# Scores and probability transposes of two pairs of heads at a time, both as 64-row products in double PSUM banks

## The chip, the cores and the metric

The kernel runs on one core of one Trainium2 chip. The metric is the device time of one execution in microseconds, as a median of several runs. The engines are TensorE (PE, with its weight loads as PEld), VectorE (DVE), ScalarE (ACT), GpSimd (POOL) and SyncE (SP), which issues nearly all DMAs.

## What is computed

Two layers of a decoder, 256 tokens, width 1024, float32. Each layer normalises its input, projects it with one 1024 x 9808 matrix, runs three causal attention mixers of eight heads of 64 (a: plain causal, b: only the 64 keys that an indexer selects per query, c: with a forgetting bias), gates and projects each, merges them by gates, projects once more and adds to the residual; a last RMSNorm ends it.

```python
h = rms_norm(x, gain)
proj = jnp.einsum('bsd,de->bse', h, w_in)
...
rel = jax.nn.relu(jnp.einsum('bqhd,bsd->bqhs', qi, k_idx))
isc = jnp.einsum('bqh,bqhs->bqs', wi, rel).astype(jnp.float32)
ival, idx = lax.top_k(isc, top)
...
s = jnp.einsum('bqhd,bkhd->bhqk', qc, kh).astype(jnp.float32) * scale
p = jax.nn.softmax(s, axis=-1).astype(v.dtype)
return jnp.einsum('bhqk,bhkd->bqhd', p, vh)
...
merged = jnp.sum(gates * y, axis=2)
return x + jnp.einsum('bsd,de->bse', merged, w_out)
```

## The kernel before

Every float32 matmul with weights is done as three products of split operands: high part by high part, high by low and low by high. ACT makes the high part of a weight block (`wh`, L371), DVE the low part (`wl`, L375), both into rings of six. A unit of projection is 24 matmuls of 128 x 256 into one PSUM bank of a ring of three (`proj`, L419). Units of gates and output projections (`unit_m`, `unit_y`) are strewn among those of the mixers by `between`, so that PE has other work while a softmax runs.

The work is not issued in the order in which it is written. Each `pe`, `act`, `dve`, `gps` and `dma` call adds an operation to a `Plan`, with its dependences, a key and a cost in ns. `Plan.run` walks through them, always takes the engine that can start earliest and there the ready operation with the lowest key, and emits it: so the costs (`QK` and numbers in the calls), a margin of 200 ns on some PE operations, and the numbers of buffers set each engine's order, which is then fixed. Buffers of one name are handed out in the order in which they were made.

Heads go in pairs, since two heads of 64 fill 128 partitions. For a pair, `scores` (L579 to L591) makes twelve products: for the first 128 queries against 128 keys, then for the next 128 against 256 keys, three split products each, for both heads in turn; one head uses rows 0 to 63 of PE, the other rows 64 to 127, and each its own PSUM bank (`s`, two banks). Then DVE adds the bias and takes a maximum (L650), ACT makes the exponentials (L654), DVE a reciprocal (L657), DVE or ACT the normalisation (L664, L661). The probabilities of a head, 128 x 384, are turned by three 128 x 128 transposes on PE (L676) into a bank of `t` (two banks). ACT copies them out as the high part (`pth`, L679), DVE makes the low part (`ptl`, L681); of both there is one buffer for a pair. Four matmuls a head (L693 to L696) then weigh the values into `o`, one bank. The indexer's four pairs of heads use `scores` too, followed by a ReLU on ACT (L805) and sums on DVE (L816).

A mixer's units of a half (two pairs) come as q, q, g, g, k, k: after a key unit its pair's attention is queued (`attend`). At the end, `forms` (L1070) issues sixteen transposes of 64 rows, two at a time for the two halves of PE, whose results nobody reads.

## Time and profile before

| | us |
|---|---|
| median of 3 runs | 608.72 (608.58 to 608.77) |
| profiled execution, its own time | 609.18 |
| its span, first to last instruction | 607.4 |
| PE busy | 600.0 |
| DVE busy | 525.5 |
| ACT busy | 401.0 |
| granted TensorE clock | 0.998 |

Busy times are unions of an engine's instruction times. Matmuls overlap, so what one costs is read from start to start. The chain of waits follows the work that ended last back to its beginning; idle time of an engine outside it costs nothing.

### The profile page before, as it was taken

Reading aid. Unit: us, or ns where it says so; the run is one execution under the profiler, and the core shown is the slowest. Engines: PE = TensorE matmul, PEld = TensorE weight load, DVE = VectorE, ACT = ScalarE, POOL = GpSimd, SP = SyncE. Lnnn points to the kernel's source line nnn. Section 1 sums busy time; section 2 is a strip of 40 time slices with the busy share of each in tenths; the row PEclk is TensorE's granted clock in tenths of the full one; section 3 lists DMA queues with packets and bytes.
Section 4 is the critical chain, followed back from the end, with each engine's and each line's share of the span. In section 5 each row is a group of like instructions: output and inputs, shape, how many; then the busy total and the mean of one; then the engine's idle time right before and its main releaser. Section 6 shows DMA issues by size and latency. Waiting matters only on the chain.

```text
span 607.4 us, 12894 instructions
## 1 busy us (share of the span) xinstructions
PE 600.0 (99%) x5036; PEld 576.3 (95%) x5036; DVE 525.5 (87%) x1227; ACT 401.0 (66%) x813; POOL 85.1 (14%) x98
## 2 busy tenths in 40 slices
PE   9999999999999999999999999999999999999996
PEld 8999999989998999999889999999999999999995
DVE  6799999787889989979588899987869898999783
ACT  6785568495777667775587563957768674858641
POOL 1232022200000223200003312202000013330001
PEclk9999999999999999999999999999999999999999
DMA  9767464736472654455555828283564556453811
GB/s 306 254 209 250 139 217 160 244 105 202 146 241 73 208 175 144 153 198 201 161 175 172 278 74 253 92 281 102 184 198 147 166 175 208 140 174 105 278 36 69
DMA packets 94461, 107.68 MB, mean 177 GB/s; under 512 B 4400, under 2 KB 82496, under 8 KB 94400
## 3 DMA queue, kind: packets, MB, share of 16 engines
q1 hardware_dynamic: 94112, 106.47, 54.8%
q8 instruction: 39, 0.64, 0.4%
q10 hardware_dynamic: 288, 0.39, 0.2%
q14 instruction: 22, 0.18, 0.1%
HBM read 105.79 MB, written 1.06 MB: 176 GB/s over the span
## 4 chain that ended last, share of the span: by engine, by line
PE 89%; DVE 7%; issue 1%; ACT 1%; DMA 1%; POOL 0%; POOLq 0%; ACTq 0%; SPq 0%
PE proj L419 75%; PE s L588 4%; PE t L676 3%; DVE wl L375 2%; PE proj L973 2%; DVE isc L837 1%; DMA raw<-in_w_in_dram 1%; PE t L898 1%; DVE t L836 1%; PE o L696 1%; PE o L693 1%; ACT wh L371 1%; PE o L694 0%; PE o L695 0%; DVE isc L816 0%
## 5 line engine op out<-in xcount | busy, mean ns | idle before, releaser
L375 DVE TENSOR_TENSOR wl<-raw,wh 128x1024 fp32r<-128x1024 f32 (+1 forms) x190 | 236.3, 1252 | 37.3 <-ACT wh L371 34.4
L371 ACT ACTIVATE wh<-raw 128x1024 fp32r<-128x1024 f32 (+1 forms) x190 | 199.8, 1057 | 85.0 <-PE proj L419 53.0
L419 PE MATMUL proj<-hTh,wh 128*128 128x256 f32 (+1 forms) x1040 | 247.5, 277 | 0.0
L419 PE MATMUL proj<-hTl,wh 128*128 128x256 f32 (+1 forms) x1040 | 245.6, 275 | 0.0
L419 PEld LDWEIGHTS proj<-hTh,wh 128*128 128x128 f32 (+1 forms) x1040 | 198.9, 191 | 1.2 <-DVE g L620 0.3
L419 PEld LDWEIGHTS proj<-hTl,wh 128*128 128x128 f32 (+1 forms) x1040 | 199.0, 191 | 0.1
L419 PE MATMUL proj<-hTh,wl 128*128 128x256 f32 (+1 forms) x1040 | 161.6, 278 | 0.0
L419 PEld LDWEIGHTS proj<-hTh,wl 128*128 128x128 f32 (+1 forms) x1040 | 136.7, 191 | 2.3
L475 POOL TENSOR_TENSOR rsh<-rsh,cst 128x256 f32<-128x256 f32 (+1 forms) x42 | 33.6, 800 | 370.3 <-DVE rsh L474 361.2
L654 ACT ACTIVATE e<-e,st 128x128 f32<-128x128 f32 x96 | 42.6, 445 | 15.6 <-DVE st L650 15.1
L477 POOL TENSOR_TENSOR rr<-rr,rsh 128x256 f32<-128x256 f32 (+1 forms) x42 | 42.8, 1021 | 7.0 <-DVE rr L476 3.8
L419 PE MATMUL proj<-wh,v 128*128 128x512 f32 (+1 forms) x144 | 33.7, 356 | 0.0
L419 PE MATMUL proj<-og0l,wh 128*128 128x256 f32 x128 | 31.9, 275 | 0.0
L419 PE MATMUL proj<-og0h,wh 128*128 128x256 f32 x128 | 31.9, 275 | 0.0
L419 PE MATMUL proj<-wh,hTh 128*128 128x512 f32 x80 | 31.7, 396 | 0.0
L419 PE MATMUL proj<-wh,hTl 128*128 128x512 f32 x80 | 30.5, 382 | 0.2 <-DVE hTl L535 0.2
L419 PEld LDWEIGHTS proj<-wh,v 128*128 128x128 f32 x144 | 25.2, 190 | 2.9
L681 DVE TENSOR_TENSOR ptl<-t,pth 128x384 fp32r<-128x384 f32 x48 | 25.1, 547 | 0.6 <-ACT pth L679 0.5
L419 PE MATMUL proj<-og0h,wl 128*128 128x256 f32 x128 | 24.7, 275 | 0.0
L419 PEld LDWEIGHTS proj<-og0h,wh 128*128 128x128 f32 x128 | 24.6, 192 | 0.0
L419 PEld LDWEIGHTS proj<-og0l,wh 128*128 128x128 f32 x128 | 24.6, 192 | 0.0
L679 ACT ACTIVATE pth<-t 128x384 fp32r<-128x384 f32 x48 | 22.3, 487 | 2.7 <-PE t L676 2.6
(196 smaller groups left out, 978.1 us busy)
## 6 DMA issues: line engine op xcount, KB each, us to landing
raw<-in_w_in_dram SPq DMA_DIRECT2D x74, 1024.0 KB, 5.2
raw<-in_w_branch_dram SPq DMA_DIRECT2D x24, 512.0 KB, 3.8
raw<-in_w_out_dram SPq DMA_DIRECT2D x8, 1024.0 KB, 5.1
brow<-drow SPq DMA_DIRECT2D x4, 512.0 KB, 6.0
raw<-in_w_in_dram SPq DMA_DIRECT2D x3, 512.0 KB, 7.5
x<-in_x_dram SPq DMA_DIRECT2D x4, 256.0 KB, 3.0
raw<-in_w_in_dram SPq DMA_DIRECT2D x2, 320.0 KB, 8.8
out_dram<-tmp SPq DMA_DIRECT2D x2, 320.0 KB, 2.5
```

The costliest lines, as they stand in the source:

```text
L371: ACT.activation(p[0].v, sel(c.v), AF.Copy)
L375: DVE.tensor_tensor(p[1].v, sel(c.v), p[0].v.bitcast(F32), op=ALU.subtract)
L419: PE.matmul(o(), a(), b(), start=first and i == 0, stop=last and i == n - 1)
L475: gps(lambda: POOL.tensor_tensor(T(sh)[:np_], T(sh)[:np_], s[:np_], op=ALU.mult), S, [k_rope], [sh], key, "rope")
L477: gps(lambda: POOL.tensor_tensor(T(r)[:np_], T(r)[:np_], T(sh)[:np_], op=ALU.add), S, [sh], [r], key, "rope")
L588: PE.matmul(T(s)[:, a:a + n].rearrange("p (b a) -> p b a", a=2), st[r, sl], turns(mv[r, :n]), start=i == 0, stop=i == 2, skip_group_check= ...
L654: act(lambda t=t, a=a, n=n, e=e, st=st: ACT.activation(T(e)[:, a:a + n], T(e)[:, a:a + n], AF.Exp, bias=T(st)[:, t:t + 1], scale=-1.0, acc ...
L676: PE.transpose(T(ps)[:, i * 128:(i + 1) * 128], T(es[h])[:, i * 128:(i + 1) * 128], ident)
L679: act(lambda h=h, src=src: ACT.activation(T(ph)[:, h], src(), AF.Copy), 384, True, [ps], [kp[h][0]], key, "pT", touch=[ph])
L681: dve(lambda h=h, src=src: DVE.tensor_tensor(T(pl)[:, h], src(), T(ph)[:, h].bitcast(F32), op=ALU.subtract), 384, [ps, kp[h][0]], [kp[h][1 ...
L693: PE.matmul(o0(128), v[:, 0, hd], f(T(ph), 0), start=True, stop=False, skip_group_check=True)
L973: PE.matmul(T(ps[t]).rearrange("p (b a) -> p b a", a=2), h(2 * i + x, t), turns(v3(w)[:, x]), start=left[t][0] == 23, stop=left[t][0] == 0)
```

## The change

Two pairs are treated together. `scores` no longer queues its products: it returns them as a job, and `half_rows` queues the jobs of two pairs as one PE operation, which the planner prices at the sum of their costs plus one `SWITCH`. Within a pair, the 256-key part comes ahead of the 128-key part. The probabilities of both pairs are transposed by one such operation too, with products of 64 rows: for each 128 x 128 block, rows 0 to 63 and rows 64 to 127 are transposed in turn by the two halves of PE, 12 products a pair, into the two banks of a double bank. PSUM has two double banks `d` in place of the banks `s` and `t`; all their former users take `d`. One ACT copy and one DVE subtraction of 768 columns per pair replace two of 384. The units of a half come as q, q, k, k, g, g, and the attention of both pairs is queued after the second key unit. The indexer's four pairs go in two groups. `forms` is gone. `Bank` objects only tell the planner which engine used a bank last.

```diff
-QK = 700.0
+PARTS = ((0, 6),)
+QK = 672.0
+PT = 360.0
+SWITCH = 330.0
 FB = ("DVE",)
 FBK = 0
-BANKS = ("proj", "s", "t", "o")
+BANKS = ("proj", "o")
...
-    ptag("s", 2)
-    ptag("t", 2)
+    ptag("d", 2, 1024)
     ptag("o", 1)
...
-    def scores(q, k, ktoks, key):
-        s2 = [Buf("s"), Buf("s")]
+    def half_rows(jobs, key, name):
+
+        def go():
+            for f in fs:
+                f()
+        fs, cost, reads, writes, touch = zip(*jobs)
+        pe(go, sum(cost) + SWITCH, [r for x in reads for r in x], [w for x in writes for w in x], key, name, MARGIN,
+           touch=[t for x in touch for t in x])
+
+    def scores(q, k, toks):
+        d = Buf("d")
 
         def go():
             qh, ql = T(q[0]), T(q[1])
             kh, kl = T(k)
-            for a, n, sl in ((0, 128, slice(0, 128)), (128, 256, slice(128, 256))):
+            for a, n, sl in ((128, 256, slice(128, 256)), (0, 128, slice(0, 128))):
                 for i, (st, mv) in enumerate(((qh, kh), (ql, kh), (qh, kl))):
-                    for r, s in zip(HEAD, s2):
-                        PE.matmul(T(s)[:, a:a + n].rearrange("p (b a) -> p b a", a=2), st[r, sl], turns(mv[r, :n]),
+                    for h, r in enumerate(HEAD):
+                        c = h * 512 + a
+                        PE.matmul(T(d)[:, c:c + n].rearrange("p (b a) -> p b a", a=2), st[r, sl], turns(mv[r, :n]),
                                   start=i == 0, stop=i == 2, skip_group_check=True)
-        pe(go, QK, [q[0], q[1], k] + ktoks, s2, key, "qk", MARGIN)
-        return s2
+        return d, (go, QK, [q[0], q[1], k] + toks, [d], d.banks)
+
+    def transposes(es, ke):
+        d = Buf("d")
+
+        def go():
+            for j in range(6):
+                e = T(es[j // 3])[:, (j % 3) * 128:(j % 3 + 1) * 128]
+                for u, r in enumerate(HEAD):
+                    PE.matmul(T(d)[:, u * 512 + j * 64:u * 512 + j * 64 + 64], e[r], ident[r, r], is_transpose=True,
+                              start=True, stop=True, skip_group_check=True)
+        return d, (go, PT, ke + [k_id], [d], es + d.banks)
 
     class Pair:
...
-            self.attend(key + 1)
+            self.key = key + 1
+            if self.p % 2:
+                attend(self.both)
...
+            self.p_es, self.p_ke = es, [k for kk in ke for k in kk]
+
+        def values(self, ps, key):
             ph, pl = Buf("pth"), Buf("ptl")
-            kp = [[Tok(), Tok()] for _ in range(2)]
-            for h in range(2):
-                ps = Buf("t")
-
-                def tr(h=h, ps=ps):
-                    for i in range(3):
-                        PE.transpose(T(ps)[:, i * 128:(i + 1) * 128], T(es[h])[:, i * 128:(i + 1) * 128], ident)
-                pe(tr, 275.0, ke[h] + [k_id], [ps], key, "pT", MARGIN, touch=[es[h]])
-                src = lambda ps=ps: T(ps)[:, :384]
-                act(lambda h=h, src=src: ACT.activation(T(ph)[:, h], src(), AF.Copy), 384, True, [ps],
-                    [kp[h][0]], key, "pT", touch=[ph])
-                dve(lambda h=h, src=src: DVE.tensor_tensor(T(pl)[:, h], src(), T(ph)[:, h].bitcast(F32), op=ALU.subtract),
-                    384, [ps, kp[h][0]], [kp[h][1]], key, "pT", touch=[ph, pl])
+            kp = []
+            for a, n in PARTS:
+                src = lambda a=a, n=n: T(ps).rearrange("p (u c) -> p u c", u=2)[:, :, a * 64:(a + n) * 64].rearrange("p u (j q) -> p j u q", q=64)
+                dst = lambda x, a=a, n=n: T(x).rearrange("p h c -> p (h c)")[:, a * 128:(a + n) * 128].rearrange("p (j u q) -> p j u q", u=2, q=64)
+                k = [Tok(), Tok()]
+                kp.append(k)
+                act(lambda src=src, dst=dst: ACT.activation(dst(ph), src(), AF.Copy), 128 * n, True, [ps], k[:1], key, "pT", touch=[ph] + ps.banks)
+                dve(lambda src=src, dst=dst: DVE.tensor_tensor(dst(pl), src(), dst(ph).bitcast(F32), op=ALU.subtract), 128 * n,
+                    [ps, k[0]], k[1:], key, "pT", touch=[ph, pl] + ps.banks)
...
+    def attend(prs):
+        key = prs[-1].key
+        sc = [scores(p.q, p.k, p.kt) for p in prs]
+        half_rows([j for _, j in sc], key, "qk")
+        for p, (d, _) in zip(prs, sc):
+            p.softmax(d, p.key)
+        ts = [transposes(p.p_es, p.p_ke) for p in prs]
+        half_rows([j for _, j in ts], key, "pT")
+        for p, (d, _) in zip(prs, ts):
+            p.values(d, p.key)
...
-        s2 = scores(q, kb, ktoks, key + 1)
-        base = (p % 2) * 768
-        rel = [tmp6[:, base + h * 384:base + (h + 1) * 384] for h in range(2)]
-        for h in range(2):
-            for a, n in ((0, 128), (128, 256)):
-                act(lambda h=h, a=a, n=n: ACT.activation(plain(rel[h][:, a:a + n]), tiles(T(s2[h])[:, a:a + n]), AF.Relu), n, True, [s2[h]],
-                    [k_tmp[p % 2]], key + 1, "relu")
-        for h in range(2):
-            hd = 2 * p + h
-            for t, (a, n) in enumerate(((0, 128), (128, 256))):
-                rr = rel[h][:, a:a + n]
-                w = widx[:, t, hd:hd + 1]
-                o = isc[:, a:a + n]
-                if hd == 0:
-                    f = lambda rr=rr, w=w, o=o: DVE.tensor_scalar(o, rr, w, None, op0=ALU.mult)
-                else:
-                    f = lambda rr=rr, w=w, o=o: DVE.scalar_tensor_tensor(o, rr, w, o, op0=ALU.mult, op1=ALU.add)
-                dve(f, n, [k_tmp[p % 2], k_widx], [k_isc[t]], key + 1, "isc", t_dve(n) + 76.0, port=True)
+        held.append((p, *scores(q, kb, ktoks)))
+        if p % 2 == 0:
+            return
+        half_rows([j for _, _, j in held], key + 1, "qk")
+        for p, d, _ in held:
+            base = (p % 2) * 768
+            rel = [tmp6[:, base + h * 384:base + (h + 1) * 384] for h in range(2)]
+            for h in range(2):
+                for a, n in ((0, 128), (128, 256)):
+                    act(lambda d=d, h=h, a=a, n=n, rel=rel: ACT.activation(plain(rel[h][:, a:a + n]), tiles(T(d)[:, 512 * h + a:512 * h + a + n]),
+                                                                           AF.Relu), n, True, [d], [k_tmp[p % 2]], key + 1, "relu", touch=[d.banks[h]])
...
-                for hf in range(2) for kind in "qgk" for p in (2 * hf, 2 * hf + 1)]
+                for hf in range(2) for kind in "qkg" for p in (2 * hf, 2 * hf + 1)]
...
-    def forms():
-
-        b = [Buf("s"), Buf("s")]
-
-        def emit():
-            for i in range(8):
-                for r, s in zip(HEAD, b):
-                    PE.matmul(T(s)[:, (i % 4) * 64:(i % 4) * 64 + 64], tmp6[r, i * 128:(i + 1) * 128], ident[r, r], is_transpose=True,
-                              start=True, stop=True, skip_group_check=True)
-        pe(emit, 900.0, [k_main] + k_tmp, b, 10 ** 6, "forms")
-    forms()
```

The planner orders the engines anew. PE, first layer, the first mixer's second half (`L419` and `L428` are projections, `L588` and `L609` scores, `L676` and `L620` transposes); before, the transposes of one pair's two heads and the beginning of the next pair's scores:

```order
L419 MATMUL proj_165<-hTh,wl_70 128x256 x4
L676 MATMUL t_170<-cst,e_136 128x128 x3
L419 MATMUL proj_166<-wh_64,hTh 128x512
L419 MATMUL proj_166<-wh_64,hTl 128x512
L419 MATMUL proj_166<-wh_64,hTh 128x512
L419 MATMUL proj_166<-wh_64,hTl 128x512
L419 MATMUL proj_166<-wl_71,hTh 128x512 x2
L676 MATMUL t_169<-cst,e_137 128x128 x3
L588 MATMUL s_167<-k0h,qh_87 128x128
L588 MATMUL s_168<-k0h,qh_87 128x128
L588 MATMUL s_167<-k0h,ql_90 128x128
L588 MATMUL s_168<-k0h,ql_90 128x128
```

The two heads' transposes stood apart, with projections between, and the next pair's scores behind them. Now, on PE too, the scores of both pairs:

```order
L609 MATMUL d_168<-k3h,qh_86 128x256 x2
L609 MATMUL d_168<-k3h,ql_89 128x256 x2
L609 MATMUL d_168<-k3l,qh_86 128x256 x2
L609 MATMUL d_168<-k3h,qh_86 128x128 x2
L609 MATMUL d_168<-k3h,ql_89 128x128 x2
L609 MATMUL d_168<-k3l,qh_86 128x128 x2
L609 MATMUL d_167<-k0h,qh_87 128x256 x2
L609 MATMUL d_167<-k0h,ql_90 128x256 x2
L609 MATMUL d_167<-k0l,qh_87 128x256 x2
L609 MATMUL d_167<-k0h,qh_87 128x128 x2
L609 MATMUL d_167<-k0h,ql_90 128x128 x2
L609 MATMUL d_167<-k0l,qh_87 128x128 x2
```

The second pair's scores have moved ahead of the first pair's transposes and stand right behind the first pair's. 48 projection matmuls later on PE come the transposes (`e_136` and `e_137` are the first pair's two heads):

```order
L428 MATMUL proj_164<-hTh,wl_70 128x256 x4
L620 MATMUL d_168<-cst,e_136 128x64 x6
L620 MATMUL d_168<-cst,e_137 128x64 x6
L620 MATMUL d_167<-cst,e_138 128x64 x6
L620 MATMUL d_167<-cst,e_139 128x64 x6
L428 MATMUL proj_166<-hTh,wh_68 128x256
```

The four heads' transposes, six products each, have moved together. ACT at the same place (`L654` and `L687` are exponentials, `L371` and `L380` weight copies, `L679` and `L712` copies of the transposes); before:

```order
L654 ACTIVATE e_136,st_144<-e_136,st_144 128x128
L654 ACTIVATE e_136,st_144<-e_136,st_144 128x256
L654 ACTIVATE e_137,st_145<-e_137,st_145 128x128
L661 ACTIVATE e_136<-e_136,st_144 128x256
L654 ACTIVATE e_137,st_145<-e_137,st_145 128x256
L405 ACTIVATE k0h<-rr_128 128x256
L661 ACTIVATE e_137<-e_137,st_145 128x256
L679 ACTIVATE pth<-t_170 128x384
L853 ACTIVATE mth_163<-proj_165 128x256
L371 ACTIVATE wh_68<-raw_123 128x1024
L679 ACTIVATE pth<-t_169 128x384
L371 ACTIVATE wh_63<-raw_123 128x1024
```

One pair's exponentials were followed by its own copies. ACT now, at the same place:

```order
L687 ACTIVATE e_136,st_144<-e_136,st_144 128x256
L687 ACTIVATE e_137,st_145<-e_137,st_145 128x128
L687 ACTIVATE e_137,st_145<-e_137,st_145 128x256
L687 ACTIVATE e_138,st_146<-e_138,st_146 128x128
L687 ACTIVATE e_138,st_146<-e_138,st_146 128x256
L687 ACTIVATE e_139,st_147<-e_139,st_147 128x128
L687 ACTIVATE e_139,st_147<-e_139,st_147 128x256
L653 ACTIVATE th_131<-proj_165 128x256
L380 ACTIVATE wh_66<-raw_125 128x1024
L380 ACTIVATE wh_67<-raw_125 128x1024
L903 ACTIVATE mth_162<-proj_164 128x256
L712 ACTIVATE pth<-d_168 128x768
```

The exponentials of both pairs now stand together, ahead of the first copy of the transposes, with a gate's tanh, two weight copies and another tanh between.

More of the change, by code (lines that the diff above doesn't have):

```diff
@@ L94, in __init__ @@
         self.tag, self.left, self.slot, self.end = tag, 0, None, 0.0
-        self.no, self.last = None, None
+        self.no, self.last, self.banks = None, None, [Bank(), Bank()]
+class Bank:
+    last = None
 class Op:
     __slots__ = ("ways", "deps", "bufs", "new", "key", "n", "out", "need", "eng", "end", "lag", "name", "start",
-                 "margin", "port")
+                 "margin", "port", "banks")
 class Plan:
@@ L115, in op @@
         deps, o.bufs = {}, []
+        o.banks = [t for t in touch if isinstance(t, Bank)]
         for t in reads:
@@ L167, in run @@
                     tt = max(t, free.get(e, 0.0))
-                    for b in o.bufs:
+                    for b in o.bufs + o.banks:
                         if b.last is not None and b.last.eng != e:
@@ L200, in run @@
             done += 1
+            for b in o.banks:
+                b.last = o
             for b in o.bufs:
@@ L249, in tag, with ptag @@
         plan.tag(name, [pool.tile(shape, dt, name=f"{name}{i}") for i in range(n)])
-    def ptag(name, n):
-        plan.tag(name, [psum.tile([128, 512], F32, name=f"{name}{i}") for i in range(n)])
+    def ptag(name, n, cols=512):
+        plan.tag(name, [psum.tile([128, cols], F32, name=f"{name}{i}") for i in range(n)])
     def T(b):
@@ L525, in norm_to_hT @@
                 sl = (slice(None), c, slice(t * 128, (t + 1) * 128))
-                src = lambda ps=ps, k=k: T(ps)[:, k * 128:(k + 1) * 128]
+                src = lambda at_cols=at_cols, k=k: at_cols(k)
                 g = gT[:, l, c:c + 1]
                 act(lambda sl=sl, src=src, g=g: ACT.activation(hTh[sl], src(), AF.Copy, scale=g), 128, True,
-                    [ps, k_gT], [k_hT[0][t][c]], key, "hT", 93.0)
+                    [ps, k_gT], [k_hT[0][t][c]], key, "hT", 93.0, touch=at)
             for k in range(2):
@@ L536, in norm_to_hT @@
                     hTl[sl], src(), g, hTh[sl].bitcast(F32), op0=ALU.mult, op1=ALU.subtract), 128,
-                    [ps, k_gT, k_hT[0][t][c]], [k_hT[1][t][c]], key, "hT", t_dve(128) + 61.0)
+                    [ps, k_gT, k_hT[0][t][c]], [k_hT[1][t][c]], key, "hT", t_dve(128) + 61.0, touch=at)
     def final_part(t, c, n, i, key, on_dve):
@@ L595, in __init__ @@
             self.mixer, self.p, self.vi, self.oi = mixer, p, vi, oi
+            self.both = None
         def ev_q(self, ps, key):
@@ L638, in bias, with softmax @@
             return (lambda: T(b)), kb, [b]
-        def attend(self, key):
+        def softmax(self, d, key):
             bs = [self.bias(h, key) for h in range(2)]
-            s2 = scores(self.q, self.k, self.kt, key)
             es, ke = [], []
@@ L647, in attend @@
                 kt = [Tok(), Tok()]
-                parts = ((0, 0, 128, s2[h]), (1, 128, 256, s2[h]))
+                parts = ((0, 0, 128, d), (1, 128, 256, d))
                 for t, a, n, s in parts:
                     dve(lambda t=t, a=a, n=n, s=s, e=e, st=st, b=b, h=h: DVE.tensor_tensor_reduce(
-                        plain(T(e)[:, a:a + n]), tiles(T(s)[:, a:a + n]), plain(b()[:, a:a + n]), 1.0, 3e38, ALU.add, ALU.min,
-                        T(st)[:, t:t + 1]), n, [s, bt[t]], [kt[t]], key, "max", t_dve(n) + 9.0, touch=[e, st] + bb)
+                        plain(T(e)[:, a:a + n]), tiles(T(s)[:, 512 * h + a:512 * h + a + n]), plain(b()[:, a:a + n]), 1.0, 3e38, ALU.add, ALU.min,
+                        T(st)[:, t:t + 1]), n, [s, bt[t]], [kt[t]], key, "max", t_dve(n) + 9.0, touch=[e, st, s.banks[h]] + bb)
                 for t, a, n, s in parts:
@@ new lines, in index_scores @@
+        if p % 2 == 0:
[8 more added lines that the diff above has]
+                                                                           AF.Relu), n, True, [d], [k_tmp[p % 2]], key + 1, "relu", touch=[d.banks[h]])
+            for h in range(2):
+                hd = 2 * p + h
+                for t, (a, n) in enumerate(((0, 128), (128, 256))):
+                    rr = rel[h][:, a:a + n]
+                    w = widx[:, t, hd:hd + 1]
+                    o = isc[:, a:a + n]
+                    if hd == 0:
+                        f = lambda rr=rr, w=w, o=o: DVE.tensor_scalar(o, rr, w, None, op0=ALU.mult)
+                    else:
+                        f = lambda rr=rr, w=w, o=o: DVE.scalar_tensor_tensor(o, rr, w, o, op0=ALU.mult, op1=ALU.add)
+                    dve(f, n, [k_tmp[p % 2], k_widx], [k_isc[t]], key + 1, "isc", t_dve(n) + 76.0, port=True)
@@ L895, in hybrid_trunk @@
     DVE.memset(half, -0.5)
-    warm = plan.tags["t"][0][1]
+    warm, spare = plan.tags["d"][0][1], plan.tags["o"][0][1]
     for _ in range(WARM):
@@ L979, in first_v @@
             v_out(ps[t], t, 0, done[t], us[t])
-        idle = Buf("o")
         for i in range(10):
-            pe(lambda: PE.matmul(T(idle)[:, :128], ones, ones, start=True, stop=True), 215.0, done[0][:1], [idle], 10 ** 5, "warm")
+            pe(lambda: PE.matmul(spare[:, :128], ones, ones, start=True, stop=True), 215.0, done[0][:1], [], 10 ** 5, "warm")
     def pair_unit(l, m, pr, kind, p):
@@ L990, in mixer @@
         prs = [Pair(m, p, vi, oi) for p in range(4)]
+        for p in range(4):
+            prs[p].both = prs[p // 2 * 2:p // 2 * 2 + 2]
         return [lambda kind=kind, p=p: pair_unit(l, m, prs[p], kind, p)
-                for hf in range(2) for kind in "qgk" for p in (2 * hf, 2 * hf + 1)]
+                for hf in range(2) for kind in "qkg" for p in (2 * hf, 2 * hf + 1)]
     def m_of(l, n, gates, js):
```

20 lines of the change are left out of this document (12 added, 8 removed).

## The prediction

> **What bounds the kernel now.** I read the page first: the shares of the engines, the slices, and the chain that ended last.
>
> ```profile
> span 607.4 us, 12894 instructions
> PE 600.0 (99%) x5036; PEld 576.3 (95%) x5036; DVE 525.5 (87%) x1227; ACT 401.0 (66%) x813; POOL 85.1 (14%) x98
> PEclk9999999999999999999999999999999999999999
> PE 89%; DVE 7%; issue 1%; ACT 1%; DMA 1%; POOL 0%; POOLq 0%; ACTq 0%; SPq 0%
> ```
>
> TensorE (PE) holds 89% of the chain, at full clock throughout. A busy PE could still be one that waits inside a matmul, so I looked next at what PE's own rows waited for.
>
> ```profile
> PE s L1077 <- ACT tmp L569: 2.6, 1, 2.6
> PE t L898 <- DVE half L895: 1.1, 1, 1.1
> PE t L676 <- DVE e L664: 0.3, 1, 0.3
> PE s L588 <- ACT k1h L405: 0.3, 1, 0.3
> PE proj L419 <- DVE hTl L535: 0.2, 1, 0.2
> ```
>
> These are all its waits (us in total, times, longest). The first two stand at the very end and at the very start; in between PE lost 0.8 us. So the kernel is a dense row of matmuls, and a microsecond taken out of PE's row is a microsecond of the span, unless a wait takes its place. The price of a step must be read from start to start, since durations overlap (a projection matmul "lasts" 0.28 us and the next starts after 0.11).
>
> **Scores.** One pair of heads, with projections on both sides (columns: start, us to the end of the row's last, count):
>
> ```profile
> 117.43 0.28 PE L419 MATMUL proj<-hTh,wh 128*128 128x256 f32 x1
> 117.77 0.28 PE L419 MATMUL proj<-hTl,wh 128*128 128x256 f32 x1
> 117.97 0.33 PE L588 MATMUL s<-k3h,qh 64*128 64x128 f32 x2
> 118.13 0.28 PE L588 MATMUL s<-k3h,ql 64*128 64x128 f32 x2
> 118.24 0.28 PE L588 MATMUL s<-k3l,qh 64*128 64x128 f32 x2
> 118.36 0.33 PE L588 MATMUL s<-k3h,qh 64*128 64x256 f32 x2
> 118.52 0.28 PE L588 MATMUL s<-k3h,ql 64*128 64x256 f32 x2
> 118.63 0.28 PE L588 MATMUL s<-k3l,qh 64*128 64x256 f32 x2
> 118.84 0.71 PE L419 MATMUL proj<-hTh,wl 128*128 128x256 f32 x4
> 119.39 0.28 PE L419 MATMUL proj<-hTh,wh 128*128 128x256 f32 x1
> ```
>
> Three projections in a row take 0.34 us (117.43 to 117.77), 0.113 each. From 117.77 to 119.39 are 1.62 us, of which five projections are 0.565: the pair costs 1.055 us. Where it goes: into the 64-row products 0.09 (0.20 for a step of 0.11); six steps of about 0.112, each of which starts both heads; 0.05 on top at the first step; 0.05 on top where the output grows from 128 to 256 columns (118.36 to 118.52); out again 0.10 (0.21 at the last step) and 0.10 more in the four projections behind (0.55 for 0.45). So 0.29 us of each pair is the change from 128 rows to 64 and back.
>
> The changed kernel does two pairs in one visit, and in each the 256 columns first. Twelve steps are 1.34 us, in and out 0.29, the first step 0.05, and one growth from 128 to 256, between the pairs, 0.05: 1.73 us against 2.11. There are 32 pairs (in each of two layers four of the indexer and twelve of the mixers), so 16 visits, and 16 x 0.38 = **6.1 us** less. Bounds: if a change from 256 to 128 columns costs 0.05 too, which no row shows, two more in each visit take back 1.6 us; if none costs, 0.8 more is saved.
>
> **Transposes.** Before: three products of 128 rows for a head, in the array's full height like the projections around them. After: the same data as 64-row products, two at once. That form stands in the trace once, in L1077, whose results nobody reads. The rows of both:
>
> ```profile
> L676 PE MATMUL t<-cst,e x144: 272/273/329, 87.1 to 556.0; 128*128 128x128 f32 x144
> 93.76 0.61 PE L419 MATMUL proj<-hTh,wl 128*128 128x256 f32 x4
> 94.21 0.49 PE L676 MATMUL t<-cst,e 128*128 128x128 f32 x3
> 94.65 0.28 PE L419 MATMUL proj<-hTl,wh 128*128 128x256 f32 x1
> 603.64 0.71 PE L1077 MATMUL s<-cst,tmp 64*128 64x64 f32 x16 [2.57 <-ACT tmp L569]
> 603.76 0.41 PE L1077 MATMUL s<-cst,tmp 64*128 64x64 f32 x8
> 604.13 0.23 PE L1077 MATMUL s<-cst,tmp 64*128 64x64 f32 x2
> ```
>
> From 93.76 to 94.65 (0.89 us) run five projections (0.565) and three transposes: 0.33 for a head, 1.31 for the four heads of two pairs, and no loss at either side. L1077's second pair of products starts at 603.76 and its eighth at 604.13: 0.062 a step, and 0.12 for the first. Two pairs of heads are 24 products, twelve steps: 0.74, plus 0.05 at the first, plus 0.29 for going in and out, if this costs what it costs the scores: 1.08 us. The 144 transposes make 12 such groups; 12 x 0.23 = **2.8 us** less. Bounds: if in and out cost nothing, as before, 3.5 us more are saved; if a step took a score step's 0.112, the form would lose 0.6 x 12 = 7.2. I take 0.062, the only row of this form, and 0.29, the nearest change of rows.
>
> The Trainium skill, "TensorEngine Tiling (Array Packing)", Key Properties, says that changing the tiling mode drains TensorE; this speaks against the edit, since 128-row transposes cause no change and the new ones cause two per group. The 0.09 and 0.20 above agree with it. The same page, Theoretical Speedup, allows up to 2x for 64 rows; by that the twelve steps would take half of 1.31, an estimate of 0.65 instead of 0.74, and the forecast below would be 1.0 us lower; L1077's 0.062 decides against it.
>
> **Around PE.** The copies out of PSUM become half as many of twice the length.
>
> ```profile
> L371 ACT ACTIVATE wh<-raw 128x1024 fp32r<-128x1024 f32 (+1 forms) x190 | 199.8, 1057 | 85.0 <-PE proj L419 53.0
> L681 DVE TENSOR_TENSOR ptl<-t,pth 128x384 fp32r<-128x384 f32 x48 | 25.1, 547 | 0.6 <-ACT pth L679 0.5
> 119.29 0.28 DVE L650 CUSTOM_DVE_ANT_0 e<-s,cst 128x128 f32<-128x128 f32 x1
> 119.58 0.39 ACT L853 ACTIVATE mth<-proj 128x256 f32<-128x256 f32 x1 [2.71 <-PE proj L419]
> 119.87 0.39 ACT L654 ACTIVATE e<-e,st 128x128 f32<-128x128 f32 x1
> 120.25 0.49 ACT L654 ACTIVATE e<-e,st 128x256 f32<-128x256 f32 x1
> 120.74 0.39 ACT L654 ACTIVATE e<-e,st 128x128 f32<-128x128 f32 x1
> 122.35 0.29 DVE L664 TENSOR_SCALAR e<-e,st 128x128 f32<-128x128 f32 x1
> 122.76 0.47 ACT L679 ACTIVATE pth<-t 128x384 fp32r<-128x384 f32 x1
> ```
>
> 128 more columns cost ACT 0.10 here (0.39 to 0.49), so 384 more make its copy about 0.77 us; on DVE it takes less than twice 0.55, and I take 1.0 (estimates). Neither engine has more to do than before, and this is off the path. Removing L1077 brings nothing: PE ends it at 604.35 while the output, below, is under way until about 606.3.
>
> ```profile
> 603.62 0.35 ACTq L573 DMA_DIRECT2D out_dram<-tmp  x1
> out_dram<-tmp ACTq DMA_DIRECT2D x2, 192.0 KB, 2.3
> ```
>
> The change adds one wait: a group of transposes waits for the softmax of **both** pairs, and all later projections stand behind it on PE. For one pair the rows give 119.29 to 122.64, 3.35 us from the first maximum to the end of a normalisation. The second pair adds four exponentials, 0.38 and 0.49 apart in turn: 1.74. With 0.4 us from the last score to the first maximum (118.91 to 119.29) and 0.2 for the signal to PE (an estimate, half of that) it is 5.7 us. The new order on PE has 48 projections in between where there are fewest (the second group of mixer a, 5.4 us, and 0.2 for leaving the scores), 56 in four groups (6.3 us) and 64 to 76 in the others (512 columns counted as two). So one group is about on time, four have 0.8 us to spare, the rest more. Behind it comes the weighted sum, which needs both copies. At that place ScalarE's order has two tanh and two weight copies, 2 x 0.39 + 2 x 1.06 = 2.9 us, between the last exponential and the first copy. The exponentials end some 1.0 us before the transposes can start (reciprocal, normalisation, signals), so the copies begin about 1.9 us after that start and end, with 0.77, 1.0 and the signals, at about 4.0; PE comes there after the transposes and 24 projections, 0.8 + 0.2 + 2.7 = 3.7. Such places have no reserve; I add 0.1 us for each of the 12 groups, **1.2 us**. The next scores need both PSUM tiles free; between the later pair's weighted sum and the next scores are 42 projections or more (4.7 us), which hides it. The move of the gate units behind the key units is the same PE work in another order, and is part of that cover.
>
> **The sum.** The profiled execution took 609.18 us (span 607.4), 0.46 above the median of 608.72. It becomes 609.18 - 6.1 - 2.8 + 1.2 = 601.5; by the median, **601.0 us**.
>
> **Rivals.**
>
> *The softmax of the second pair takes the place of what was saved (slower).* If PE stood at all 12 groups for the second pair's whole 1.74 us, that is 20.9: 608.7 - 8.9 + 20.9 = 620.7. It decides from 0.74 us a group (8.9 / 12). For it: eight exponentials now stand together on ScalarE, with weight copies behind them. Against: 48 to 76 projections of cover, and only 0.3 us of such a wait before.
>
> *DVE binds while the indexer selects.*
>
> ```profile
> 60.00:80.00 20.00, 20.00 (x181) 20.00 (x181) 20.00 (x68) 9.33 (x15) 1.47 (x2) 1.00 0.57 184
> 80.00:100.00 20.00, 19.72 (x183) 18.78 (x183) 19.92 (x59) 17.93 (x44) 4.74 (x6) 1.00 0.45 135
> 360.00:380.00 20.00, 20.00 (x184) 19.76 (x183) 20.00 (x61) 9.10 (x15) 3.04 (x4) 1.00 0.65 202
> ```
>
> After the stretch's length stand the busy us of PE, PEld, DVE, ACT and POOL: DVE is full in both layers' selection. What PE saves up to there (three visits of scores and one of transposes per layer, 2 x (3 x 0.38 + 0.23) = 2.7) would come back as waits for weights: 603.7. Against: PE hardly waited in it, and selection can run later.
>
> *The new transposes don't overlap* (0.112 a step): 601.0 + 7.2 = 608.2, no change; L1077 speaks against. *They go in and out at no cost*, as the old ones did: 601.0 - 3.5 = 597.5; only an idle engine has shown this form, so no row excludes it.
>
> **How the numbers follow.** Forecast, 599 to 603: 0.66. DVE or part of the softmax binding, 603 to 606: 0.17. Free change of rows, 599 and below: 0.06. No overlap, within 0.2%: 0.05 with what comes near it by waits. Slower by waits: 0.06. The range 597.5 to 605 leaves out the two last and the ends. A measurement of this kernel tells about 0.2% (1.2 us) from no change. Faster 0.89, same 0.05, slower 0.06.
>
> **What would show it.** Right: one visit of scores from the last projection to the next in 1.7 us; steps of 0.062 in the transposes; PE's waits for the normalised tiles and for the split copies of the transposes under 2 us. Wrong: a step of 0.11 there, more than 0.05 lost inside a visit, PE waiting over 0.5 us at most groups, or waits for split weights in the two selection stages.

## The result and the profile after

| | before | after |
|---|---|---|
| median, us | 608.75 (608.58 to 609.62, 4 runs) | 601.97 (601.86 to 602.42, 4 runs) |
| ratio | 1 | 0.9887 (95%: 0.987 to 0.9904) |
| span of the profiled execution, us | 607.4 | 600.3 |
| PE / DVE / ACT busy, us | 600.0 / 525.5 / 401.0 | 590.1 / 526.0 / 386.1 |
| granted TensorE clock | 0.998 | 0.997 |

The change makes the kernel 6.8 us faster by the medians and 7.1 by the spans. The forecast was 601.0, its range 597.5 to 605.0: right in sign and cause, 1.0 us too low. Two of its terms were off by as much or more, in opposite senses, and that they nearly cancel is luck. One execution named below differs in kind: e2's profiled one took 1236 us, with 0.22 us between projections in place of 0.11, and is left out of e2's median, so that e11 gives the trace.

In the profile after, the head of the page, the chain that ended last, and the longest waits of PE (us in total, times, longest):

```profile
span 600.3 us, 13137 instructions
PE 71%; DVE 24%; issue 3%; ACT 2%; POOL 0%; POOLq 0%; ACTq 0%
```

```profile
PE d L948 <- DVE half L945: 1.0, 1, 1.0
PE o L725 <- DVE ot L743: 0.9, 2, 0.4
PE proj L428 <- DVE wl L384: 0.6, 1, 0.6
PE d L609 <- DVE k1l L415: 0.5, 1, 0.5
PE proj L1023 <- DVE hTl L546: 0.3, 1, 0.3
```

(In the changed code L428 is the projections, L609 the scores, L620 the transposes, L384 the low parts of weights, L415 of other operands, L713 the low part of the probabilities, L743 the evacuation of `o`.) DVE's share of the chain went from 7% to 24%, and the longest waits of PE are all for DVE (the first of them, at the very start, stands in both kernels). Before, only one wait of 0.3 us between start and end was put down to DVE's softmax, and 0.2 to its `hTl`.

**The scores**, one visit of two pairs in the trace's order of time (start, us to the end of the row's last, count):

```profile
112.46 0.61 PE L428 MATMUL proj<-hTh,wl 128*128 128x256 f32 x4
113.00 0.38 PE L609 MATMUL d<-k3h,qh 64*128 64x256 f32 x2
113.22 0.27 PE L609 MATMUL d<-k3h,ql 64*128 64x256 f32 x2
...
113.44 0.22 PE L609 MATMUL d<-k3h,qh 64*128 64x128 f32 x2
113.50 0.28 PE L609 MATMUL d<-k3h,ql 64*128 64x128 f32 x2
...
113.72 0.33 PE L609 MATMUL d<-k0h,qh 64*128 64x256 f32 x2
113.88 0.28 PE L609 MATMUL d<-k0h,ql 64*128 64x256 f32 x2
...
114.28 0.28 PE L609 MATMUL d<-k0l,qh 64*128 64x128 f32 x2
114.48 0.38 PE L428 MATMUL proj<-hTh,wh 128*128 128x256 f32 x1
114.70 0.28 PE L428 MATMUL proj<-hTl,wh 128*128 128x256 f32 x1
```

From 112.46 to 114.70 are 2.24 us; five projections in it are 0.56. The visit costs 1.68, in the median of all 16 it is 1.676. Two single visits cost 2 x 1.060 before (32 of them, median). So the scores save 0.444 x 16 = **7.1 us**. The step from 256 to 128 columns (113.44 to 113.50) takes only 0.06. No run undoes the new order of the units (q, k, g) by itself, so its share of what follows can't be told apart.

**The transposes** of two pairs:

```profile
119.50 0.61 PE L428 MATMUL proj<-hTh,wl 128*128 128x256 f32 x4
120.04 0.97 PE L620 MATMUL d<-cst,e 64*128 64x64 f32 x24
120.94 0.38 PE L428 MATMUL proj<-hTh,wh 128*128 128x256 f32 x1
121.15 0.28 PE L428 MATMUL proj<-hTl,wh 128*128 128x256 f32 x1
```

From 119.50 to 121.15 are 1.65 us; less five projections, the group costs 1.09 where the old ones took 1.31: 0.22 x 12 = **2.6 us**. The two gains are 9.7, and the span fell by 7.1. Some 2.6 us were given back as waits: 0.9 ahead of the first 128 x 256 projection, which starts at 22.53 for 21.61, and 1.7 behind it, since from there to the last one PE takes 571.2 for 579.2. The experiments ask where.

**Where they were given back.** I compared each step of PE, from start to start, with the usual step between two instructions of the same kinds. Three kinds of place stand out. The first is the start. After, all engines in order of time:

```profile
7.57 0.88 ACT L539 ACTIVATE hTh<-d,gT 128x128 fp32r<-128x128 f32 x3
...
8.49 0.35 DVE L546 SCALAR_TENSOR_TENSOR hTl<-d,gT,hTh 128x128 fp32r<-128x128 f32 x1
...
8.87 1.40 ACT L539 ACTIVATE hTh<-d,gT 128x128 fp32r<-128x128 f32 x5 [0.42 <-DVE hTl L546]
8.96 0.42 PE L1023 MATMUL proj<-wh,hTl 128*128 128x512 f32 x1
9.27 0.87 DVE L546 SCALAR_TENSOR_TENSOR hTl<-d,gT,hTh 128x128 fp32r<-128x128 f32 x3 [0.44 <-ACT hTh L539]
9.68 0.48 PE L1023 MATMUL proj<-wh,hTl 128*128 128x512 f32 x1 [0.30 <-DVE hTl L546]
```

and the same place before:

```profile
8.10 0.63 ACT L528 ACTIVATE hTh<-s,gT 128x128 fp32r<-128x128 f32 x2
8.24 0.61 DVE L535 SCALAR_TENSOR_TENSOR hTl<-t,gT,hTh 128x128 fp32r<-128x128 f32 x2 [0.32 <-ACT hTh L528]
...
8.77 0.60 DVE L535 SCALAR_TENSOR_TENSOR hTl<-s,gT,hTh 128x128 fp32r<-128x128 f32 x2
8.97 0.59 PE L973 MATMUL proj<-wh,hTl 128*128 128x512 f32 x2
```

Before, ACT copies out of one bank while DVE reads the other, and neither idles. After, ACT and DVE wait for each other in turn (0.42, 0.44), and PE's step at 8.96 takes 0.72 in place of 0.22. By then, and by what it delays, the ninth matmul of L1023 starts 4.69 us after the first, where before it was 3.84, and the projections behind are 0.9 us late.

The second is the two selection stages. Here in the first layer, on PE, ACT and DVE:

```profile
71.35 0.51 ACT L414 ACTIVATE k1h<-rr 128x256 fp32r<-128x256 f32 x1 [3.20 <-POOL rr L486]
...
72.39 0.60 DVE L886 MAX8 t<-isc 128x8 f32<-128x128 f32 x2
...
72.55 0.28 PE L609 MATMUL d<-k1h,ql 64*128 64x256 f32 x2
72.91 0.40 DVE L415 TENSOR_TENSOR k1l<-rr,k1h 128x256 fp32r<-128x256 f32 x1
...
73.36 0.38 PE L609 MATMUL d<-k1l,qh 64*128 64x256 f32 x2 [0.54 <-DVE k1l L415]
73.58 0.22 PE L609 MATMUL d<-k1h,qh 64*128 64x128 f32 x2
```

The high part of a key is done at 71.86, and DVE could make its low part (0.40). It first works off selection rounds that stand ahead of it in its order, until 72.91, and PE's step at 72.55 takes 0.81 in place of 0.11. Likewise PE's steps at 91.79 (for `ptl`, 0.46 in place of 0.06) and at 391.22 (for a low part of a weight, 0.92 in place of 0.11).

The third is the one bank `o` in mixer b, in each layer once; the first of them:

```profile
230.32 1.74 DVE L384 TENSOR_TENSOR wl<-raw,wh 128x1024 fp32r<-128x1024 f32 x1
...
230.94 1.71 POOL L484 TENSOR_TENSOR rsh<-rsh,cst 128x256 f32<-128x256 f32 x1
...
231.99 0.94 DVE L713 TENSOR_TENSOR ptl<-d,pth 128x768 fp32r<-128x768 f32 x1
...
232.85 0.83 DVE L743 SCALAR_TENSOR_TENSOR ot<-o,ot 64x256 f32<-64x256 f32 x2
...
233.83 0.35 PE L725 MATMUL o<-pth,v 128*128 128x256 f32 x1 [0.41 <-DVE ot L743]
```

The second pair's weighted sum needs `o`, which DVE has yet to empty for the first pair. The sums of two pairs now stand 3.3 to 4.6 us apart, where before it was 5.2 or more, and DVE has the low part of a weight and the second pair's `ptl` between. PE's steps at 233.14 and 525.12 take 0.69 and 0.72 for 0.11. No run gives `o` a second bank, so that this would remove the wait is not shown. All in all, with a start after each wait that is some 0.1 longer, these places cost 0.9 + 0.8 + 0.4 + 0.9 + 2 x 0.67 = 4.3 us, and two smaller ones at 384.12 and 393.60 another 0.3. The waits of before, at 80.5, 87.5, 175.7, 381.4, 391.0 and 471.8, came to 2.0 by the same steps and are gone: 4.6 - 2.0 is the 2.6.

By place it looks otherwise than by length. The start gave back 0.9 and the bank `o` in mixer b 1.3, where before there was nothing. The selection stages hold 2.4 us of waits, but before they held 1.6 (80.5, 87.5, 381.4, 391.0), so they gave back only 0.8; 0.4 elsewhere is gone.

### The profile page after: what moved, and what is told of

The parts are those of the page before. It is cut to its first block, busy times and chain, and to the rows that moved or that the text cites. A ratio compares the mean times of both kernels' runs of the same rounds, so it can differ in the third digit from the quotient of the medians.

```text
span 600.3 us, 13137 instructions
## 1 busy us (share of the span) xinstructions
PE 590.1 (98%) x5164; PEld 568.9 (95%) x5164; DVE 526.0 (88%) x1232; ACT 386.1 (64%) x758; POOL 91.2 (15%) x100
## 4 chain that ended last, share of the span: by engine, by line
PE 71%; DVE 24%; issue 3%; ACT 2%; POOL 0%; POOLq 0%; ACTq 0%
PE proj L428 62%; DVE wl L384 9%; PE d L609 2%; PE proj L1023 2%; DVE isc L887 2%; DVE e L683 1%; DVE t L886 1%; DVE rsh L483 1%; PE d L620 1%; DVE ptl L713 1%; DVE e L697 1%; DVE isc L865 1%; PE d L948 1%; ACT wh L380 1%; DVE rr L485 1%
## 5 line engine op out<-in xcount | busy, mean ns | idle before, releaser
L384 DVE TENSOR_TENSOR wl<-raw,wh 128x1024 fp32r<-128x1024 f32 (+1 forms) x190 | 240.3, 1282 | 27.5 <-ACT wh L380 22.6
L428 PE MATMUL proj<-hTh,wh 128*128 128x256 f32 (+1 forms) x1040 | 247.1, 277 | 0.0
L428 PE MATMUL proj<-hTl,wh 128*128 128x256 f32 (+1 forms) x1040 | 245.8, 276 | 0.0
L380 ACT ACTIVATE wh<-raw 128x1024 fp32r<-128x1024 f32 (+1 forms) x190 | 197.6, 1054 | 72.9 <-PE proj L428 40.2
L428 PEld LDWEIGHTS proj<-hTh,wh 128*128 128x128 f32 (+1 forms) x1040 | 199.0, 191 | 0.9
L428 PEld LDWEIGHTS proj<-hTl,wh 128*128 128x128 f32 (+1 forms) x1040 | 199.4, 192 | 0.2
L428 PE MATMUL proj<-hTh,wl 128*128 128x256 f32 (+1 forms) x1040 | 160.5, 277 | 0.6 <-DVE wl L384 0.6
L428 PEld LDWEIGHTS proj<-hTh,wl 128*128 128x128 f32 (+1 forms) x1040 | 136.8, 191 | 1.7 <-DVE wl L384 0.8
L484 POOL TENSOR_TENSOR rsh<-rsh,cst 128x256 f32<-128x256 f32 (+1 forms) x42 | 36.3, 866 | 314.8 <-DVE rsh L483 309.5
L687 ACT ACTIVATE e<-e,st 128x128 f32<-128x128 f32 x96 | 42.3, 442 | 17.7 <-DVE st L683 17.7
L486 POOL TENSOR_TENSOR rr<-rr,rsh 128x256 f32<-128x256 f32 (+1 forms) x42 | 46.7, 1116 | 10.1 <-DVE rr L485 5.6
L428 PE MATMUL proj<-wh,v 128*128 128x512 f32 (+1 forms) x144 | 33.7, 357 | 0.0
L428 PE MATMUL proj<-og0l,wh 128*128 128x256 f32 x128 | 31.9, 276 | 0.0
L428 PE MATMUL proj<-og0h,wh 128*128 128x256 f32 x128 | 31.9, 275 | 0.0
L428 PE MATMUL proj<-wh,hTl 128*128 128x512 f32 x80 | 30.6, 383 | 0.2 <-DVE hTl L546 0.2
L428 PE MATMUL proj<-wh,hTh 128*128 128x512 f32 x80 | 30.8, 385 | 0.0
L712 ACT ACTIVATE pth<-d 128x768 fp32r<-128x768 f32 x24 | 19.3, 803 | 17.0 <-PE o L726 15.0
L713 DVE TENSOR_TENSOR ptl<-d,pth 128x768 fp32r<-128x768 f32 x24 | 22.9, 952 | 7.7 <-ACT pth L712 7.6
L428 PEld LDWEIGHTS proj<-wh,v 128*128 128x128 f32 x144 | 25.3, 190 | 2.9
L428 PE MATMUL proj<-og0h,wl 128*128 128x256 f32 x128 | 24.8, 275 | 0.0
L428 PEld LDWEIGHTS proj<-og0l,wh 128*128 128x128 f32 x128 | 24.6, 192 | 0.0
L428 PEld LDWEIGHTS proj<-og0h,wh 128*128 128x128 f32 x128 | 24.6, 192 | 0.0
```

What stands on the lines that cost most here:

```text
L380: ACT.activation(p[0].v, sel(c.v), AF.Copy)
L384: DVE.tensor_tensor(p[1].v, sel(c.v), p[0].v.bitcast(F32), op=ALU.subtract)
L428: PE.matmul(o(), a(), b(), start=first and i == 0, stop=last and i == n - 1)
L484: gps(lambda: POOL.tensor_tensor(T(sh)[:np_], T(sh)[:np_], s[:np_], op=ALU.mult), S, [k_rope], [sh], key, "rope")
L486: gps(lambda: POOL.tensor_tensor(T(r)[:np_], T(r)[:np_], T(sh)[:np_], op=ALU.add), S, [sh], [r], key, "rope")
L687: act(lambda t=t, a=a, n=n, e=e, st=st: ACT.activation(T(e)[:, a:a + n], T(e)[:, a:a + n], AF.Exp, bias=T(st)[:, t:t + 1], scale=-1.0, acc ...
```

## Experiments

Times are medians beside runs of the kernel before on the same chip, of which the difference is taken; the change is 6.8 us below it.

**e1: the order of columns alone.** The kernel before, with the 256-key part first.

```diff
-            for a, n, sl in ((0, 128, slice(0, 128)), (128, 256, slice(128, 256))):
+            for a, n, sl in ((128, 256, slice(128, 256)), (0, 128, slice(0, 128))):
```

> The kernel before, with the 256-key part of each pair's scores ahead of the 128-key part and nothing else changed. Theory A (steps are paid as they are on PE: the step where the output grows from 128 to 256 columns costs 0.05 us more, and it now stands nowhere inside a pair): 32 pairs x 0.05 = 1.7 us faster, about 607.0. Theory B (the order of the two parts is free, all of the gain is from shared visits): 608.7, no change.

608.04 us against 608.99, ratio 0.9982 (0.9973 to 0.9991). A pair's visit is 1.006 us in the trace, 0.054 less than 1.060: 32 x 0.054 = 1.7 us on PE, of which 0.95 reached the time. This lies between the two theories: the price on PE is that of A, the time is not. From the first 128 x 256 projection to the last, PE's row is 1.2 shorter; its first one started 0.3 later in this execution (21.88 for 21.61), and waits such as those at 80.8, 380.8 and 390.4 are each some 0.05 longer. So on PE the order is worth 1.7 of the 7.1 us of the scores; the joint visit is worth the rest, 16 x (2 x 1.006 - 1.676) = 5.4.

**e6: joint visits undone.** The change, with a visit of its own for each pair's scores.

```diff
-        half_rows([j for _, j in sc], key, "qk")
+        for _, j in sc:
+            half_rows([j], key, "qk")
...
-        half_rows([j for _, _, j in held], key + 1, "qk")
+        for _, _, j in held:
+            half_rows([j], key + 1, "qk")
```

> The changed kernel, where each pair's scores are a visit of their own (going in and out of 64-row products 16 times more), all else as in the change. Theory A (a visit costs 0.29 us for going in and out and 0.05 for its first step): 16 x 0.34 = 5.4 us slower than the changed kernel, 607.4. Theory B (the change of rows is hidden by other waits): less than 2 us slower, under 604.

610.03 us against 609.02, ratio 1.001 (0.9999 to 1.002): the whole gain is gone, 7.8 us, where theory A had 5.4. The executions lie far apart, 608.2 to 611.0, and the profiled one (608.74) is among the faster. The experiment is not clean. In five of the sixteen places both visits still stood side by side (1.676 for the two); the eleven others were 22 visits, of 1.006 where PE did not wait inside. That is 11 x 0.336 = 3.7 us. The other 2.9 of the span's 6.6 are waits of a new order, above all:

```profile
PE d L609 <- DVE k3l L415: 1.8, 1, 1.8
PE proj L428 <- DVE mth L936: 1.7, 2, 0.9
```

The price of a visit agrees with e1; the total says how much any new order can add.

**e2 and e11: the transposes at full height.** The change, with the transposes of two pairs in one group, but as products of 128 rows.

```diff
-PT = 360.0
+PT = 654.0
...
-        pe(go, sum(cost) + SWITCH, [r for x in reads for r in x], [w for x in writes for w in x], key, name, MARGIN,
+        pe(go, sum(cost) + (SWITCH if name == "qk" else 0.0), [r for x in reads for r in x], [w for x in writes for w in x], key, name, MARGIN,
...
-                for u, r in enumerate(HEAD):
-                    PE.matmul(T(d)[:, u * 512 + j * 64:u * 512 + j * 64 + 64], e[r], ident[r, r], is_transpose=True,
-                              start=True, stop=True, skip_group_check=True)
+                c = (j // 3) * 512 + (j % 3) * 128
+                PE.transpose(T(d)[:, c:c + 128], e, ident)
...
```

(The copies read and write the blocks in their new places.)

> The changed kernel, with the transposes of two pairs still in one group but as twelve products of 128 rows. Theory A (a group of 64-row products costs 1.09 us with its change of rows, twelve full-height ones 12 x 0.109 = 1.31): 12 x 0.22 = 2.6 us slower than the changed kernel, about 604.6. Theory B (PE is no longer what binds, so a little more PE work is hidden in waits for VectorE): within 1 us of the changed kernel, 602 to 603.

604.14 us against 608.99, ratio 0.9918 (0.9905 to 0.9932): 1.9 us of the gain are lost, nearer to A's 2.6 than to B, which allowed 1 at most. The same kernel, run once more for its trace:

> The change with the transposes of two pairs still in one group but as products of 128 rows, for its trace. Theory A (the prediction's terms): a group of twelve such products takes 1.31 us with no loss on entry or exit, against 1.09 measured for the 64-row group, and PE waits at the same places as in the change. Rival B (grouping alone costs, the 64 rows do not matter): the group takes 1.1 or less, or PE's waits grow by over 1 us.

604.46 us in one run against 608.92, span 602.7, 2.4 above the change. One group:

```profile
119.98 0.28 PE L428 MATMUL proj<-hTl,wh 128*128 128x256 f32 x1
120.09 1.47 PE L620 MATMUL d<-cst,e 128*128 128x128 f32 x12
121.32 0.69 PE L428 MATMUL proj<-hTh,wl 128*128 128x256 f32 x4
121.85 0.28 PE L428 MATMUL proj<-hTh,wh 128*128 128x256 f32 x1
```

From 119.98 to 121.85 are 1.87 us, less five projections 1.31. So grouping alone saves nothing, and the two halves of PE do: 0.22 a group, 2.6 in twelve. From the first 128 x 256 projection to the last, PE takes 2.1 longer than in the change (573.3 for 571.2): of theory A the price holds, but PE does not wait at the same places, since the wait at 391 is gone and those for `o` are 0.2 shorter each.

**e3 and e3b: four tiles at the start.** The change, with the four blocks of the first rows' transposes in four PSUM tiles, not in four banks of two tiles. In e3 the tiles are d, d, proj and o; there fillers of the first units write into the bank `o` before its block is read, so part of the first rows' data is overwritten. In e3b they are d, d, proj and proj.

```diff
-        dd = [Buf("d"), Buf("d")]
+        first = l == 0 and t == 0
+        dd = [Buf(n) for n in (("d", "d", "proj", "proj") if first else ("d", "d"))]
...
```

> The changed kernel, where only the first tile's eight transposed blocks of the first layer go to four separate PSUM tiles instead of two double banks. Theory A (at the start a double bank counts as one tile, so ScalarE's and VectorE's reads of its two banks wait for each other, and the first projections run 0.9 us behind those of the kernel before): 0.9 us faster than the changed kernel, about 601.1. Theory B (the start was late by chance, through the input's transfers): 602.0, no change.

> The changed kernel, where the first tile's eight transposed blocks of the first layer go to four separate PSUM tiles (one bank of each double bank and two banks of the projections) instead of two double banks. Theory A (reads of a double bank's two halves wait for each other): the third layer of projections at the start is on time, and the end comes 0.9 us earlier than in the changed kernel, about 601.1. Theory B (the start was late through the input's transfers): 602.0.

e3: 604.04 us against 608.99, ratio 0.9925 (0.9912 to 0.9938), worse than the change. Its fillers (L1036 there) now wait for the bank's readers, ACT and DVE, and steps of PE at 9.48, 10.65 and 11.87 take 0.73, 0.79 and 0.72. It says nothing on the theory. e3b: 601.37 against 609.02, ratio 0.9874 (0.986 to 0.9887), 7.65 below the kernel before where the change is 6.8 below. PE's wait for `hTl` and the alternate idling are gone, and the later waits stay as they were (steps of 0.81 at 71.36, 0.47 at 90.59, 1.02 at 390.04). The intervals of the two ratios overlap, so the times alone do not settle it; the traces do. In e3b the ninth matmul of the first projections starts 3.84 us after the first, as before, not 4.69. So it is in every trace: 3.84 in e1, e5, e8, e9 and e10, which have no double bank there, 4.69 to 4.71 in e4, e6, e7 and e11, which have. How much of these 0.85 reaches the first 128 x 256 projection depends on how long it then waits for weights: 0.7 in e3b, 0.6 in e10, 0.2 in e9. From there on PE takes 571.3 us in e3b and 571.2 in the change. The spans differ by 1.0 because e3b's first matmul of this kind also started 0.5 earlier (7.52 for 7.99), its input having landed 0.3 earlier (4.08 for 4.40); that differs from one execution to the next.

**e4 and e5: half of the selection.** The change (e4) and, as a control, the kernel before (e5), with four of the eight selection rounds left out.

```diff
-        for r in range(8):
+        for r in range(4):
```

> The changed kernel with four of the eight rounds of the indexer's selection left out, which frees VectorE of half of that work in both selection stages. Theory A (VectorE binds there: PE's waits of 0.7, 0.35 and 0.8 us in the two stages come from its queue): they go, 1.5 to 2 us faster than the changed kernel, 600.0 to 600.5. Theory B (the waits come from the longer groups on PE, whatever VectorE does): 602.0, no change.

> The kernel before with four of the eight rounds of the indexer's selection left out, as a control for the same edit of the changed kernel. Theory A (before, PE bound all the way and VectorE hardly mattered): at most 0.6 us faster than the kernel before, 608.2 to 608.9. Theory B (VectorE cost the kernel before as much as it costs the changed one): 1.2 us faster, 607.6.

e4: 600.89 us against 608.99, ratio 0.9864 (0.9851 to 0.9878), 1.3 us more gain than the change, a little under A's 1.5 to 2. e5: 608.14 against 609.02, ratio 0.9988 (0.9979 to 0.9996), 0.9 less than the kernel before, between A's 0.6 and B's 1.2. In e4 PE's waits at 72.5 and 391 are gone, but others came at 82.3, 82.8 (for normalised tiles, 0.4 each) and 91.3 (0.3). With less to do, DVE costs both kernels less, and the difference between the two, 0.4, is within the intervals. This pair alone does not settle whether DVE's load or its order costs the time.

**e7: a larger margin for PE's late operands.**

```diff
-MARGIN = 200.0
+MARGIN = 500.0
```

> The changed kernel with the planner's reserve ahead of scores, transposes and weighted sums raised from 200 to 500 ns. Theory A (PE waits at these places because the order leaves nothing in reserve): the waits there, 1.9 us in sum, mostly go, 600.5 to 601. Theory B (VectorE's queue is what is late, and the waits only move to other matmuls): 602, no change.

606.15 us against 609.02, ratio 0.9954 (0.9941 to 0.9968): 3.9 us of the gain gone, which neither theory had foreseen. The profiled execution, 604.56, is the fastest of the five and lost 2.5 of them. Its trace has the place, PE and DVE in the first selection stage:

```profile
69.33 0.28 PE L428 MATMUL proj<-hTl,wh 128*128 128x256 f32 x1
...
70.66 0.61 DVE L886 MAX8 t<-isc 128x8 f32<-128x128 f32 x2
...
71.51 1.21 DVE L384 TENSOR_TENSOR wl<-raw,wh 128x1024 fp32r<-128x1024 f32 x1
...
72.78 0.49 PE L428 MATMUL proj<-hTh,wl 128*128 128x256 f32 x2 [3.18 <-DVE wl L384]
```

In the change DVE makes this low part, the 17th of L384, at 58.14, ahead of all selection rounds. With more margin the plan puts it behind six of them, and PE stands 3.2 us for it. The work on DVE is the same as in the change: its order in this stage is worth microseconds.

**e9 and e10: the selection moved back.** e3b, with the due times of the eight rounds 3 or 2.5 units apart instead of 2.

```diff
-                select(u + 3, 2.0)
+                select(u + 3, 2.5)
```

> The change with four tiles for the first rows' transposes (601.4 us in its own run), and the due times of the eight selection rounds 3 units apart instead of 2, so that the splits of keys and weights come ahead of them in DVE's order. Theory A (what is lost in the two selection stages is DVE's order there, not DVE's load): PE's waits for a split key at about 71.4 and for a split weight at about 390.0, 0.7 and 0.9 us, go, and with them some 1.4 to 2.0 us: 599.4 to 600.0. Rival B (DVE is full there, so what is put ahead makes something else late): the time stays within 0.5 us of 601.4, with waits at other places of these stages, for instance for the selection's result.

> As the run before it, with 2.5 units between the selection rounds. Theory A: 599.4 to 600.4, by the same waits. Rival B: within 0.5 us of 601.4. If the two runs differ by over 1 us from each other, it is the particular order that counts and neither the load nor the due times as such.

e9 (3): 600.69 us against 608.92, ratio 0.9863 (0.985 to 0.9876). e10 (2.5): **600.0**, ratio 0.9849 (0.9834 to 0.9864), 8.9 below the kernel before and 1.3 further than e3b, whose interval it overlaps by a little. From the first 128 x 256 projection to the last, PE takes 569.8 us in e10 and 570.6 in e9, for 571.3 in e3b. The longest waits of e10 (its lines from L524 on are 5 higher than in the change):

```profile
PE o L730 <- DVE ot L748: 0.8, 2, 0.4
PE proj L1028 <- ACT hTh L544: 0.7, 1, 0.7
PE o L732 <- DVE ptl L718: 0.4, 1, 0.4
```

Its wait for `hTh` stands at 7.2, ahead of the place that e3b mended: in that execution ACT had waited 0.66 us for the first weights from DMA. The waits for a split key and a split weight are gone in both, without less work for DVE. Part of that came back at other places: in e9 1.5 us at 85.6 and 90.5 (steps of 0.90 and 0.74, for `ptl` and for the evacuated bank), in e10 1.1 at 80.8 and 84.6 (for a normalised tile and for `ptl`, steps of 0.37 and 0.64). So e9, 0.7 below e3b, met neither theory's number, and e10 met A's. The order alone regained as much as half of the load did in e4, 1.3 us; the runs do not rank the two. e10 is faster than the kernel before and the change; its interval is clear of both.

**e8: the unread products alone.** The kernel before without `forms`.

```diff
-    forms()
```

> The kernel before without the unread products at its end (L1077), and nothing else. Theory A (the prediction's term of 0): the output of the last rows is under way when PE ends them, so the time stays within 0.3 us of the kernel before's. Rival B: the core's end stands behind PE's end; the time falls by 0.5 to 1.5 us.

608.85 us against 608.92, ratio 1.0001 (0.9992 to 1.001): worth nothing that shows, as forecast.

## Why the prediction was right, and where it was not

*What bounds.* Right: PE's row got 9.9 us shorter in busy time (0.7 of it the unread products) and the span 7.1. With it DVE's share of the chain grew. The table of waits understated what PE lost before: it was read as 0.8 us between start and end, and by steps it is 2.0.

*Scores, 6.1 us: measured 7.1.* The mechanism held; the visit was mis-sized, 1.73 for 1.676. I let both steps from 256 to 128 columns cost an ordinary 0.11, and bounded the unknown with a loss of 0.05 or with the growth between the pairs costing nothing. They take 0.06 each, and the growth costs its 0.05 (113.72 to 113.88). Against that, the first step costs 0.1 on top at 256 columns (113.00 to 113.22), not 0.05. -0.11 + 0.05 makes up the 0.055 between 1.73 and 1.676, 0.9 us over 16 visits; the rest is rounding. A drop in columns gives back what a growth takes; I had priced only the growth.

*Transposes, 2.8 us: measured 2.6.* Right in every part: 0.09 going in (120.04 where an ordinary step would give 119.94), steps of 0.062, and out again 0.09 at the last step and 0.10 behind. The Trainium skill, "TensorEngine Tiling (Array Packing)", Key Properties, says that a change of mode drains TensorE; the trace agrees in that each change of rows costs time, 0.29 us for both ways. The cheaper case without that price (597.5) and the one without overlap (608.2) are both excluded by these rows, and e11 shows the same for the form itself.

*Copies.* Expected about 0.77 on ACT and 1.0 on DVE:

```profile
L712 ACT ACTIVATE pth<-d 128x768 fp32r<-128x768 f32 x24 | 19.3, 803 | 17.0 <-PE o L726 15.0
L713 DVE TENSOR_TENSOR ptl<-d,pth 128x768 fp32r<-128x768 f32 x24 | 22.9, 952 | 7.7 <-ACT pth L712 7.6
```

0.80 and 0.95. *The unread products* at nothing: right (e8).

*The added waits, 1.2 us: measured 2.6, mostly at other places.* This is the step that failed. It set 0.1 at each of the twelve groups: the transposes wait for two softmaxes, and the weighted sums behind them need both copies. None of the twelve groups of transposes waited over 0.1 us for a softmax: the cover of 48 to 76 projections was enough. The sums did wait, but in few places and mostly for something else: once for `ptl` (0.4, at 91.79), and three times for the bank `o`, which is emptied late (1.3 in mixer b and 0.2 at 384.12). That `o` is one bank for two pairs that now come together is not in the sum at all. Nor is DVE's order. The end of the prediction names waits for split weights in the selection stages as a sign against it, and there was one, and one for a split key; net of what the kernel before lost there, these stages cost 0.8. It wrote that the need for both PSUM tiles was hidden, which holds for the scores; it did not ask what else uses the new tiles. The first rows' transposes do, when nothing covers them yet (0.9 us at the start of the change, gone in e3b's trace).

*Rivals.* The slower one, the second pair's softmax exposed, needed 0.74 us a group; the rows show under 0.1. DVE binding in the selection was right in its place and too large in its size: it was to take back 2.7 us, and PE's waits there went from 1.6 to 2.4. e7, e9 and e10 show that DVE's order matters in it; what share is order and what is load stays open, as e4 with e5 left it.

## What to carry to other kernels

Price a joint visit by steps, each kind of transition for itself, and the falling ones too. Then ask of each merged buffer who else uses it, above all at the start, where nothing covers a wait. When PE's row gets denser, look at the fixed order of the engine that is nearly full: an item that is due sooner may stand behind work that could wait, and moving that work brought 1.3 us here (e3b to e10, by the medians) without removing any.
